# Turning the first mixer's sparse-attention queries and keys through VectorE and memory

## The chip, the cores and the metric

The kernel runs on one core of one Trainium2 chip. A core has five engines with queues of their own: TensorE (PE, matrix products into PSUM; PEld is its weight load), VectorE (DVE), ScalarE (ACT), GpSimd (POOL) and SyncE (SP, which issues transfers). The metric is the device time of one launch in microseconds, as a median of runs: 1248.22 us before, from runs of 1247.68, 1248.22 and 1251.99 us.

## The reference

A decoder trunk of two layers over 256 tokens of width 1024, in float32. Each layer is

```
x <- x + 1/2 * SwiGLU(RMSNorm(x))
h  = RMSNorm(x);  z = h @ W_in
  A: stick-breaking attention (8 heads)
  B: multi-head latent attention, MLA (8 heads of 64 + 32)
  C: native sparse attention, NSA (8 query heads of 64, 2 key groups)
y  = sum_i sigmoid(gate_i(h)) * (branch_i @ P_i)
x <- x + y @ W_out
x <- x + 1/2 * SwiGLU(RMSNorm(x))
```

Branch C is what the change touches. Its queries (512 columns of z), its selected keys (128) and its window keys (128) are each divided by their root mean square per head of 64, multiplied by a gain and rotated by position. Three attentions then use the queries: over 15 compressed keys, over the selected blocks and over a window. At 256 tokens all four blocks of 64 are selected and the window of 512 reaches over everything, so the last two are causal attentions with different keys.

## The kernel before

The 256 tokens lie as two row blocks of 128 (`NT = 2`, t = 0 and 1). Every matrix product in full precision is made of three products of a high and a low half (`mm3`, L588 to L590): ScalarE copies a value to a rounded type (the high half), VectorE subtracts (the low half). Weights go the same way (L1042, L1044). They arrive as slabs of 128 x 1024 through SP.

A layer is `ffn`, `mixer`, `ffn`. In the mixer the order of the work on TensorE, VectorE and ScalarE is written out by a planner (`Planner.run`): some twenty Python generators ask for an engine, with a cost, a latency, the events they depend on and the buffers they need, and the planner always emits the request that can start first, shifted by a fixed number per generator (`HOLDS`). The engines then run their lists in order. A request with the engine "-" costs nothing and takes only buffers or events. The costs are estimates in the code; transfers are estimated by a constant that is added to an event's time. POOL's transfers stand in POOL's list in the order in which they are emitted, and POOL also computes the powers for the root mean squares (L595).

The queries and keys of branch C lie in `nx[t]`, 128 tokens x 768 (eight query heads, then two selected and two window keys of 64). `nsa_prep` normalises and rotates them there (L1760 to L1780). For the attention products they must lie with the head's 64 numbers on the partitions and the tokens along the row. `nsa_T` does this for each row block: ScalarE writes a copy `kd` in which every key stands twice (L1888), so that a pair of query heads, which sits on partitions 0 to 63 and 64 to 127, finds its key on both halves; TensorE transposes the four query pairs (L1893) and the four doubled keys (L1902) against an identity into PSUM; ScalarE and VectorE split the results into `nq` and `nk` (L1068, L1070 in `t_split`). It waits for `ev_mqk`, the last MLA transposes, because `nq` and `nk` are taken from the ring of six big tiles (tag `hy`) that also holds MLA's `mq` and `mk`. The readers are `cmp_scores` (the product of `nq` with the compressed keys, L588 to L590 acc<-nq) and `nsa_scores` (L2036).

MLA already has another way of turning: `turn` (L1245) lets VectorE transpose a row block in place in squares of 32 x 32 and POOL write it to memory in four transfers (L1247), and `turned` (L1255) reads it back into a half tile `st` with the wanted rows on the partitions. The list `by_dve` says where: in the first mixer for `mk`, in the second for `mq` and `mk`. Half tiles come from a ring of seven (`TH_BUFS`, planner's `s_th`), which also holds gates, outputs and the copies `kd`.

Of the kernel before, what the change touches and what calls it, by code (L numbers as in the profile page):

```python
# [10 lines left out]
F = mybir.dt.float32  # L11
# [6 lines left out]
S = 256  # L18
# [3 lines left out]
NT = 2  # L22
# [203 lines left out]
def event():  # L226
    return Tok(None)
# [80 lines left out]
def use_v(n, *deps, slots=()):  # L308

    return "V", 0.065 + 0.00106 * n, 0.15 + 0.00106 * n, deps, slots  # L310
# [7 lines left out]
def use_a(n, *deps, slots=()):  # L318

    return "A", 0.085 + 0.00085 * n, 0.19 + 0.00085 * n, deps, slots  # L320
# [13 lines left out]
def use_t(count, *deps, slots=()):  # L334

    o = 0.2 + count * 0.109
    return "P", o, o + 0.2, deps, slots


def use_g(us, *deps, slots=()):  # L340

    return "G", us, us, deps, slots
# [29 lines left out]
def decoder_trunk(ctx, tc, xt_in, wts, lcon, cst, out, depth=DEPTH):  # L372
# [8 lines left out]
    dp = ctx.enter_context(tc.tile_pool(name="dp", bufs=1, space=bass.MemoryType.DRAM))  # L381
# [6 lines left out]
    def tp_tile():  # L388
        return pb.tile([128, 512], F, tag="ps", name="tp")
# [4 lines left out]
    def big_tile(name, dt=F, shape=(128, D)):  # L394
        return hp.tile(list(shape), dt, tag="hy", name=name, bufs=6)
# [196 lines left out]
    def rstd(ss, inv, w=1, p=128):  # L592
        r = sm.tile([128, 16], F, tag="rs", name="rs")
        nc.vector.tensor_scalar(ss[:p, :w], ss[:p, :w], inv, EPS, op0=OP.mult, op1=OP.add)
        nc.gpsimd.tensor_tensor(r[:p, :w], ss[:p, :w], mh[:p, :w], op=OP.pow)  # L595
        return r
# [351 lines left out]
    def mixer(l):  # L948
# [14 lines left out]
        def half_tile(name):  # L963
            return mp.tile([128, 512], F, tag="th", name=name, bufs=TH_BUFS)

        def tmp(n=768):
            return mp.tile([128, 768], F, tag="tmp", name="tmp", bufs=1)[:, :n]
# [9 lines left out]
        def bc(a, H):  # L977
            return a[:, None, :].to_broadcast([a.shape[0], H, a.shape[-1]])
# [17 lines left out]
        s_wf, s_wr, s_qk, s_th, s_tmp, s_of = Slots(4), Slots(WR_BUFS), Slots(4), Slots(TH_BUFS), Slots(1), Slots(1)  # L996

        def events(*n):
            return [events(*n[1:]) for _ in range(n[0])] if n else event()
# [65 lines left out]
        def t_split(hi, lo, src, n, k):  # L1065

            k = yield use_a(n, k)
            nc.scalar.activation(hi, src, AF.Copy)  # L1068
            k = yield use_v(n, k)
            nc.vector.tensor_sub(lo, src, hi)  # L1070
            return k
# [170 lines left out]
        def turn(x, t, dst, n, k):  # L1242

            k = yield "V", 0.065 + 0.00116 * n, 0.15 + 0.00116 * n, (k,), ()
            nc.vector.transpose(x[:, 0:n], x[:, 0:n])  # L1245
            for i in range(4):
                nc.gpsimd.dma_start(dst[:, :, t * 128 + 32 * i:t * 128 + 32 * (i + 1)],  # L1247
                                    x[32 * i:32 * (i + 1), 0:n].rearrange("b (m a) -> b m a", a=32))
            return Tok(k.t + 6.0)

        def turned(dst, parts):

            st = half_tile("st")
            for r, m, step, c in parts:
                nc.gpsimd.dma_start(st[32 * r:32 * (r + 1), c * S:(c + 2) * S].rearrange("b (j n) -> b j n", j=2),  # L1255
                                    dst[:, m:m + step + 1:step, :])
            return st
# [125 lines left out]
        side = {"_uq": side_uq, "_ukv": side_ukv, "w1_slab": lambda: compress()}  # L1383

        nx = [mp.tile([128, 768], F, name=f"nx{t}") for t in range(NT)]
        zc = []
        ev_nx, ev_zc, ev_v0 = events(NT, 2), events(NT), events(NT)

        def ev_nq(t, acc, k):
            k = yield use_a(512, k)  # L1390
# [364 lines left out]
        def nsa_prep():  # L1755
            for t in range(NT):
                x = nx[t].rearrange("p (h d) -> p h d", h=12)
                k = yield use_a(768, *ev_nx[t], slots=(s_tmp,))
                sq = tmp()
                nc.scalar.activation(sq, nx[t], AF.Square)  # L1760
                k = yield use_v(768, k)
                ss = sm.tile([128, 16], F, tag="ss", name="ss")
                nc.vector.tensor_reduce(ss[:, 0:12], sq.rearrange("p (h d) -> p h d", h=12), axis=AX.X, op=OP.add)
                k = yield "V", 0.07, 0.15, (k,), ()
                r = rstd(ss, 1.0 / 64, w=12)
                k = yield use_g(2.5, k)
                k = yield use_v(768, k)
                nc.vector.tensor_tensor(x, x, r[:, 0:12, None].to_broadcast([128, 12, 64]), op=OP.mult)
                b = tmp().rearrange("p (h d) -> p h d", h=12)
                for nm, hs_ in (("nq", slice(0, 8)), ("nk", slice(8, 12))):  # L1770
                    n = 64 * (hs_.stop - hs_.start)
                    xh, bh, H = x[:, hs_], b[:, hs_], hs_.stop - hs_.start
                    c, s_ = tab[nm][0][:, t, :], tab[nm][1][:, t, :]
                    for o, i in ((0, 32), (32, 0)):
                        k1 = yield use_v(n // 2, k)
                        nc.vector.tensor_tensor(bh[:, :, o:o + 32], xh[:, :, i:i + 32], bc(s_[:, o:o + 32], H), op=OP.mult)
                    k1 = yield use_v(n, k1)
                    nc.vector.tensor_tensor(xh, xh, bc(c, H), op=OP.mult)
                    k = yield use_v(n, k1)
                    nc.vector.tensor_tensor(xh, xh, bh, op=OP.add)  # L1780
                s_tmp.put(k)
                ev_prep[t].set(k)

        def gates():
# [95 lines left out]
        nq = tuple(big_tile("nq", R, (128, 4, S)) for _ in range(2))  # L1880
        nk = tuple(big_tile("nk", R, (128, 2, 2, NT, 128)) for _ in range(2))
        ev_nT = events(NT)

        def nsa_T():
            for t in range(NT):
                k = yield use_a(512, ev_prep[t], slots=(s_th,))
                kd = half_tile("kd").rearrange("p (a r d) -> p a r d", a=4, r=2)
                nc.scalar.activation(kd, nx[t][:, 512:768].rearrange("p (a d) -> p a d", a=4)[:, :, None, :]  # L1888
                                     .to_broadcast([128, 4, 2, 64]), AF.Copy)
                kt = yield use_t(4, ev_prep[t], *((*ev_mq, *ev_mk) if all(by_dve) else (ev_mqk,)), slots=(s_tp,))  # L1890
                tp = tp_tile()
                for p in range(4):
                    nc.tensor.transpose(tp[:, p * 128:(p + 1) * 128], nx[t][:, p * 128:(p + 1) * 128], ident)  # L1893
                ts = slice(t * 128, (t + 1) * 128)
                kt = yield from t_split(nq[0][:, :, ts], nq[1][:, :, ts], tp.rearrange("p (a b) -> p a b", a=4), 512, kt)
                s_tp.put(kt)
                k = yield use_t(4, k, slots=(s_tp,))
                tp = tp_tile()
                for g in range(2):
                    for sw in range(2):  # L1900
                        i = 2 * g + sw
                        nc.tensor.transpose(tp[:, i * 128:(i + 1) * 128],  # L1902
                                            kd[:, 2 * sw + g].rearrange("p a d -> p (a d)"), ident)
                s_th.put(k)
                k = yield from t_split(nk[0][:, :, :, t, :], nk[1][:, :, :, t, :],
                                       tp.rearrange("p (g s k) -> p g s k", g=2, s=2), 512, k)
                s_tp.put(k)
                ev_nT[t].set(k)

        def flat(pair):  # L1910
            return tuple(q.rearrange("p g r n -> p (g r n)") for q in pair)
# [230 lines left out]
        for th, hold in zip((scales(), tables(), sb_T(), sb_scores(), sb_pv(), cmp_in(), nsa_prep(), gates(), mla_T(),  # L2142
                             mla_scores(), mla_P(), mla_pv(), nsa_T(), k_chain(), v_chain(), cmp_scores(), nsa_scores(),
                             nsa_P(), nsa_pv(), bulk()), HOLDS):
            spawn(th, hold)
# [18 lines left out]
    for l in range(depth):  # L2164
        ffn(l, 0)
        mixer(l)
        ffn(l, 2)
# [35 lines left out]
```

## Time and profile before

| | |
|---|---|
| median of three runs | 1248.22 us |
| the profiled execution | 1249.25 us |
| its span | 1247.4 us |
| TensorE busy | 1239.0 us |
| VectorE busy | 943.6 us |
| ScalarE busy | 789.0 us |
| POOL busy | 155.5 us |
| granted TensorE clock | 1.00 |

The span is the part of the execution that the profiler's rows cover. A row of the kind "line, engine, operation, out<-in, x count" gives the least, median and greatest duration in ns. In the waits the engine and line that stood still come first, then the one that released it, then the sum in us, the number of times and the longest. The first mixer lies at about 190 to 445 us of the span, the second at about 810 to 1064 us.

### The profile page before, as it was taken

The page shows a single profiled execution, that of the slowest core. Times are in us where ns is not written, and L with a number is a line of the kernel's source. Part 1 is how long each engine was busy: PE and PEld are TensorE (multiplying, and loading weights), DVE is VectorE, ACT ScalarE, POOL GpSimd, SP SyncE. Part 2 cuts the span into 40 slices and gives each one's busy share as a digit, 9 for nine tenths or more (in the row PEclk, how much of TensorE's full clock was granted, in tenths as well). Part 3 has the DMA queues.
Part 4 walks back from the last instruction along what each step waited for, and adds up shares of the span by engine and source line. Part 5 has one row for each costly group of instructions (what it writes and reads, how often), then busy time and mean ns, then how long its engine had stood idle before and what let it go on. Part 6 is the DMA issues. An engine that isn't in the chain of part 4 may idle for free.

```text
span 1247.4 us, 26169 instructions
## 1 busy us (share of the span) xinstructions
PE 1239.0 (99%) x9314; PEld 1158.8 (93%) x9314; DVE 943.6 (76%) x1961; ACT 789.0 (63%) x1633; POOL 155.5 (12%) x250
## 2 busy tenths in 40 slices
PE   9999999999999999999999999999999999999998
PEld 8999999888878899999999999998888889999987
DVE  7876668988898777766677776689968987776644
ACT  6665557787887566655465565577757775565542
POOL 0021201231000001211001121013330000023000
PEclk9999999999999999999999999999999999999999
DMA  8899985667645568999758999666896556677753
GB/s 273 288 328 327 334 270 184 196 209 245 207 126 182 158 218 260 319 322 339 233 196 272 330 328 324 213 211 191 280 323 236 159 157 185 189 211 244 220 169 119
DMA packets 157218, 298.59 MB, mean 239 GB/s; under 512 B 21472, under 2 KB 24416, under 8 KB 157088
## 3 DMA queue, kind: packets, MB, share of 16 engines
q1 hardware_dynamic: 143872, 258.64, 64.8%
q0 software_dynamic: 13216, 38.29, 8.4%
q8 instruction: 73, 1.20, 0.4%
q14 instruction: 57, 0.47, 0.1%
HBM read 258.32 MB, written 38.01 MB: 238 GB/s over the span
## 4 chain that ended last, share of the span: by engine, by line
PE 94%; ACT 2%; DVE 2%; DMA 1%; issue 1%; SPq 0%; DVEq 0%; ACTq 0%
PE acc L779 13%; PE acc L778 13%; PE acc L780 12%; PE acc L588 9%; PE acc L590 9%; PE acc L589 9%; PE acc L669 6%; PE acc L670 6%; PE acc L668 6%; PE acc L1204 1%; PE acc L1206 1%; PE acc L1205 1%; DMA raw<-in_wts 1%; PE att L2036 1%; ACT wf L1632 1%; PE tp L2047 1%
## 5 line engine op out<-in xcount | busy, mean ns | idle before, releaser
L536 DVE TENSOR_TENSOR vlo<-raw,vhi 128x512 fp32r<-128x512 f32 x452 | 292.6, 686 | 82.6 <-ACT vhi L535 80.4
L778 PE MATMUL acc<-hThi,vhi 128*128 128x256 f32 x1280 | 353.4, 276 | 0.0
L780 PE MATMUL acc<-hThi,vlo 128*128 128x256 f32 x1280 | 353.4, 276 | 0.0
L779 PE MATMUL acc<-hTlo,vhi 128*128 128x256 f32 x1280 | 353.4, 276 | 0.0
L535 ACT ACTIVATE vhi<-raw 128x512 fp32r<-128x512 f32 x452 | 263.5, 622 | 134.9 <-DMA raw<-in_wts 36.0
L778 PEld LDWEIGHTS acc<-hThi,vhi 128*128 128x128 f32 x1280 | 240.3, 188 | 0.0
L780 PEld LDWEIGHTS acc<-hThi,vlo 128*128 128x128 f32 x1280 | 240.2, 188 | 0.0
L779 PEld LDWEIGHTS acc<-hTlo,vhi 128*128 128x128 f32 x1280 | 240.2, 188 | 0.0
L1044 DVE TENSOR_TENSOR wlo<-raw,whi 128x512 fp32r<-128x512 f32 x216 | 141.1, 680 | 30.4 <-ACT whi L1042 28.7
L1042 ACT ACTIVATE whi<-raw 128x512 fp32r<-128x512 f32 x216 | 124.8, 616 | 47.6 <-PE acc L590 17.2
L670 PE MATMUL acc<-gh,vlo 128*128 128x256 f32 x528 | 145.7, 276 | 0.0
L668 PE MATMUL acc<-gh,vhi 128*128 128x256 f32 x528 | 145.7, 276 | 0.0
L669 PE MATMUL acc<-gl,vhi 128*128 128x256 f32 x528 | 145.7, 276 | 0.0
L588 PE MATMUL acc<-whi,hThi 128*128 128x512 f32 (+2 forms) x352 | 138.1, 392 | 0.0
L590 PE MATMUL acc<-whi,hTlo 128*128 128x512 f32 (+2 forms) x352 | 133.6, 380 | 0.2 <-DVE hTlo L610 0.2
L589 PE MATMUL acc<-wlo,hThi 128*128 128x512 f32 (+2 forms) x352 | 133.3, 379 | 0.0
L554 ACT ACTIVATE ehi<-eraw 128x512 fp32r<-128x512 f32 x60 | 37.9, 632 | 107.3 <-DMA eraw<-in_wts 105.1
L536 DVE TENSOR_TENSOR wlo<-raw,whi 128x512 fp32r<-128x512 f32 (+2 forms) x109 | 70.0, 678 | 45.7 <-ACT whi L535 45.5
L555 DVE TENSOR_TENSOR elo<-eraw,ehi 128x512 fp32r<-128x512 f32 x60 | 41.4, 690 | 81.0 <-ACT ehi L554 80.8
L535 ACT ACTIVATE whi<-raw 128x512 fp32r<-128x512 f32 (+2 forms) x109 | 63.1, 617 | 57.9 <-PE acc L590 26.4
L668 PEld LDWEIGHTS acc<-gh,vhi 128*128 128x128 f32 x528 | 99.1, 188 | 0.0
L669 PEld LDWEIGHTS acc<-gl,vhi 128*128 128x128 f32 x528 | 99.1, 188 | 0.0
(348 smaller groups left out, 2560.1 us busy)
## 6 DMA issues: line engine op xcount, KB each, us to landing
raw<-in_wts SPq DMA_DIRECT2D x764, 256.0 KB, 3.6
eraw<-in_wts SPq DMA_DIRECT2D x60, 256.0 KB, 5.5
early<-ehi POOLq DMA_DIRECT2D x60, 256.0 KB, 4.2
early<-elo POOLq DMA_DIRECT2D x60, 256.0 KB, 4.8
whi<-early SPq DMA_DIRECT2D x60, 256.0 KB, 4.4
wlo<-early SPq DMA_DIRECT2D x60, 256.0 KB, 4.6
st<-md POOLq DMA_DIRECT2D x36, 64.0 KB, 5.1
xd<-x SPq DMA_DIRECT2D x4, 512.0 KB, 2.6
```

The costliest lines, as they stand in the source:

```text
L535: nc.scalar.activation(hi[:, q], raw[:, o:o + g], AF.Copy)
L536: last_lo[0] = nc.vector.tensor_tensor(lo[:, q], raw[:, o:o + g], hi[:, q], op=OP.subtract).ins
L588: nc.tensor.matmul(o, a[0], b[0], start=start, stop=False, **kw)
L589: nc.tensor.matmul(o, a[0], b[1], start=False, stop=False, **kw)
L590: nc.tensor.matmul(o, a[1], b[0], start=False, stop=stop, **kw)
L668: nc.tensor.matmul(o, sl[0][:, w], h, start=k == 0 and c == 0, stop=False)
L669: nc.tensor.matmul(o, sl[0][:, w], l_, start=False, stop=False)
L670: nc.tensor.matmul(o, sl[1][:, w], h, start=False, stop=k == kts - 1 and c == 1)
L778: nc.tensor.matmul(o, sl[0][:, w], h, start=k == 0 and c == 0, stop=False)
L779: nc.tensor.matmul(o, sl[0][:, w], l_, start=False, stop=False)
L780: nc.tensor.matmul(o, sl[1][:, w], h, start=False, stop=k == KT - 1 and c == 1)
L1044: nc.vector.tensor_tensor(hl[1][:, c:c + m], raw[:, :m], hl[0][:, c:c + m], op=OP.subtract)
```

## The change

In the first mixer (`l == 0`) a tensor `nd` in memory is added, 32 x 24 x 256. When a row block of `nx` is prepared, VectorE transposes it in place in squares of 32 and POOL writes it to `nd` (`turn`, 768 columns, four transfers of 96 KB each). The loop of `nsa_T` with `kd` and the transposes on TensorE runs no more there. In its place `n_back` makes four loads one behind another, two for the queries and two for the keys: a half tile is filled by four transfers of 32 partitions (64 KB each, `turned`), and `t_split` writes `nq` or `nk` from it. The doubling of the keys is done by reading the same rows of `nd` twice (`r % 2`). Each load waits for the writes of both row blocks, and the wait for `ev_mqk` is gone. All four loads together set the event `ev_nT` for both row blocks. The second mixer is as before.

```
+        nd = dp.tile([32, 24, S], F, tag="nd", name="nd") if l == 0 else None
...
+                if nd is not None:
+                    k = yield from turn(nx[t], t, nd, 768, k)
+                    ev_nd[t].set(k)
...
+        def n_back(what):
+            for i in range(2):
+                k = yield "-", 0.0, 0.0, tuple(ev_nd), (s_th,)
+                if what is nq:
+                    st = turned(nd, [(r, 8 * i + r, 4, 0) for r in range(4)])
+                    src, dst = st.rearrange("p (a n) -> p a n", a=2), [q[:, 2 * i:2 * i + 2] for q in nq]
+                else:
+                    st = turned(nd, [(r, 16 + 4 * i + r % 2, 2, 0) for r in range(4)])
+                    src = st.rearrange("p (g t k) -> p g t k", g=2, t=NT)
+                    dst = [q[:, :, i] for q in nk]
+                k = yield from t_split(dst[0], dst[1], src, 512, Tok(k.t + 5.0))
+                s_th.put(k)
+                ev_back[what is nq][i].set(k)
...
         def nsa_T():
-            for t in range(NT):
+            for t in range(NT if nd is None else 0):
...
+            if nd is not None:
+                yield from n_back(nq)
+                yield from n_back(nk)
+                for ev in ev_nT:
+                    ev.set(Tok(max(e.t for x in ev_back for e in x)))
```

More of the change, by code (lines that the diff above doesn't have):

```diff
@@ L1385, in mixer @@
         nx = [mp.tile([128, 768], F, name=f"nx{t}") for t in range(NT)]
+        nd = dp.tile([32, 24, S], F, tag="nd", name="nd") if l == 0 else None
         zc = []
-        ev_nx, ev_zc, ev_v0 = events(NT, 2), events(NT), events(NT)
+        ev_nx, ev_zc, ev_v0, ev_nd = events(NT, 2), events(NT), events(NT), events(NT)
         def ev_nq(t, acc, k):
@@ L1882, in mixer @@
         ev_nT = events(NT)
+        def n_back(what):
[11 more added lines that the diff above has]
+                ev_back[what is nq][i].set(k)
+        ev_back = events(2, 2)
         def nsa_T():
-            for t in range(NT):
+            for t in range(NT if nd is None else 0):
                 k = yield use_a(512, ev_prep[t], slots=(s_th,))
```

## The prediction

> **What bounds the kernel now.** I read first the page's busy times and the chain of waits, then the stretches of both mixers, then who TensorE waited for between 240 and 345 us, and last the rows of each tile that the edit touches.
>
> ```profile
> span 1247.4 us, 26169 instructions
> PE 1239.0 (99%) x9314; PEld 1158.8 (93%) x9314; DVE 943.6 (76%) x1961; ACT 789.0 (63%) x1633; POOL 155.5 (12%) x250
> ...
> PE 94%; ACT 2%; DVE 2%; DMA 1%; issue 1%; SPq 0%; DVEq 0%; ACTq 0%
> ```
>
> TensorE is busy for all but 8.4 of 1247.4 us and is 94% of the chain. A microsecond taken from TensorE's queue is therefore worth up to a microsecond; one taken from another engine is worth something only if TensorE waits for it. In the first mixer it hardly does (columns: stretch, its length, then busy us of PE, PEld, DVE, ACT, POOL, granted clock, DMA share, GB/s):
>
> ```profile
> 280.00:300.00 20.00, 20.00 (x125) 17.86 (x124) 18.54 (x44) 14.36 (x32) 6.62 (x10) 1.00 0.80 263
> 300.00:320.00 20.00, 20.00 (x144) 17.61 (x144) 15.83 (x49) 16.97 (x47) 0.00 (x0) 1.00 0.75 236
> 320.00:345.00 25.00, 24.42 (x173) 19.88 (x172) 22.77 (x61) 20.70 (x53) 0.94 (x1) 1.00 0.54 174
> ...
> sum 240.00, PE 239.26 PEld 205.61 DVE 205.89 ACT 181.20 POOL 27.32; mean PE 34.18 PEld 29.37 DVE 29.41 ACT 25.89 POOL 3.90
> ...
> PE tp L1945 <- DVE wf L1940: 0.3, 1, 0.3
> PE tp L1673 <- ACT wf L1664: 0.2, 1, 0.2
> ```
>
> From 200 to 440 us TensorE is idle for 0.74 us, and between 240 and 345 us it waits twice, 0.5 us in all, neither time for what the edit touches. So the edit cannot free more than the TensorE work that it takes out and those 0.74 us.
>
> **Taken from TensorE: 16 transposes.** They stand in four groups of four: nx at 324.37 and 327.57, kd at 325.76 and 336.94. The modelled duration of one (272 ns) overlaps its neighbours, so I take the time from a group's start to the next matmul's start.
>
> ```profile
> 324.14 0.40 PE L590 MATMUL acc<-whi,hTlo 128*128 128x512 f32 x1
> 324.37 0.60 PE L1893 MATMUL tp<-ident,nx 128*128 128x128 f32 x4
> 324.73 0.27 PE L588 MATMUL acc<-w,hvh 128*64 128x64 f32 x1
> ...
> 327.57 0.60 PE L1893 MATMUL tp<-ident,nx 128*128 128x128 f32 x4
> 327.93 0.48 PE L588 MATMUL acc<-whi,hThi 128*128 128x512 f32 x1
> 328.25 0.40 PE L589 MATMUL acc<-wlo,hThi 128*128 128x512 f32 x1
> 328.48 0.39 PE L590 MATMUL acc<-whi,hTlo 128*128 128x512 f32 x1
> ...
> 340.49 0.39 PE L588 MATMUL acc<-nq,zkh 128*128 128x256 f32 x1
> ```
>
> One group takes 0.36 us, and the matmul behind it 0.32 in place of the usual 0.23 (328.48 less 328.25), so 0.45 in all: 4 x 0.45 = 1.8. One of the four stands ahead of small matmuls, where less is lost, so I take **-1.7 us**.
>
> **ScalarE, VectorE and the two copies.** Removed are the two doubled copies kd; the four splits now read a loaded tile instead of a PSUM bank; added are two VectorE transposes of a row block, the same instruction that turns mk already.
>
> ```profile
> L1888 ACT ACTIVATE kd<-nx x4: 620/632/633, 281.5 to 918.8; 128x512 f32<-128x512 f32 x4
> L1068 ACT ACTIVATE nq<-tp x4: 577/597/599, 325.0 to 920.6; 128x512 fp32r<-128x512 f32 x4
> L1070 DVE TENSOR_TENSOR nq<-tp,nq x4: 674/687/693, 325.6 to 921.5; 128x512 fp32r<-128x512 f32 x4
> ...
> L1068 ACT ACTIVATE qk<-st x4: 614/618/625, 287.2 to 322.6; 96x512 fp32r<-96x512 f32 x4
> L1070 DVE TENSOR_TENSOR qk<-st,qk x4: 677/682/690, 290.2 to 324.2; 96x512 fp32r<-96x512 f32 x4
> ...
> L1245 DVE STREAM_TRANSPOSE mk<-mk x4: 970/972/980, 247.6 to 891.7; 128x768 f32<-128x768 f32 x4
> ```
>
> ScalarE: 2 x 0.632 less, 4 x (0.618 - 0.597) more, so -1.2 us. VectorE: 2 x 0.972 more and the splits equal, so +1.9 us. Both are costed at nothing on the path: TensorE's own queue covers them, and it does not wait there now. If that cover were gone, VectorE's 1.9 us would be the price; it is 93% busy from 280 to 300 us, where the first transpose falls, but only 79% in the next 20 us, so a delay of 1 us is made up there. The doubled copy of the first row block held one of the seven half tiles from 281.5 us until its transposes at 325.76; the new loads hold one at a time, so that ring gets no tighter.
>
> **POOL and the transfers.** Eight writes of 96 KB and sixteen reads of 64 KB are added, all issued by POOL. Their rows are those of mk's turn in this mixer:
>
> ```profile
> L1247 POOL DMA_DIRECT2D md<-mk x8: 694/735/789, 248.9 to 263.9; - x8
> md<-mk POOLq DMA_DIRECT2D x8, 96.0 KB, 2.6
> DMA to landing us min/median/max: 2.4/2.8/6.1
> ...
> L1255 POOL DMA_DIRECT2D st<-md x12: 533/533/605, 271.9 to 297.8; - x12
> DMA to landing us min/median/max: 2.1/4.1/5.1
> ...
> 296.67 1.65 POOL L1255 DMA_DIRECT2D st<-md  x3 [4.49 <-DVE y L1452]
> 326.53 0.94 POOL L595 TENSOR_TENSOR rs<-ss,mh 64x1 f32<-64x1 f32 x1 [28.21 <-DVE ss L594]
> 330.21 0.27 DVE L1928 TENSOR_SCALAR wf<-acc,rs 64x64 f32<-64x64 f32 x1
> ```
>
> (The first landing row is mk's in both mixers, 2.4 to 6.1; the second is st's in this one.) Issuing costs POOL 8 x 0.735 + 16 x 0.533 = 14.4 us, in a stretch where it now does nothing from 298 to 326 us. What queues behind a waiting read on POOL is the load for MLA's last head pair, now issued at 296.67 and first read 26 us later (the last st split, 322.6), and the power of the compressed keys at 326.53. Behind that power stands VectorE's L1928; its slack is 330.21 - 327.47 = 2.7 us, and four issues in front of the power are 2.1 us. Both are hidden, the second barely.
>
> [...]
>
> **The new wait.** The loads go one behind another: each takes a half tile, is read, split by ScalarE and VectorE, and only then comes the next.
>
> ```profile
> 299.72 0.42 DVE L1780 TENSOR_TENSOR nx<-nx,tmp 128x256 f32<-128x256 f32 x1
> ```
>
> The second row block is ready at 300.14. Then: transpose 0.97, issues 4 x 0.735 = 2.94, landing 2.6, so 306.65 us in memory. Each of the four trips: issues 4 x 0.533 = 2.13, landing 4.1, splits 0.62 + 0.68, so 7.53. Queries are there at 321.7 and keys at 306.65 + 4 x 7.53 = **336.8 us**. The first matmul that reads them stands at 340.49, and 3 of the 4 groups removed lie ahead of it plus the last at 336.94, so it moves to about 338.8. By medians the margin is 2 us. With the longest landings seen (6.1 once, 5.1 four times) the keys come at 336.8 + 3.5 + 4 x 1.0 = 344.3, and TensorE, which runs its list in order, would wait 5.5 us. With the shortest (2.1) they come at 328.6 and nothing waits.
>
> The smaller cost is ScalarE's. The planner puts each split 5.0 us behind its load (the constant in n_back), where issue and landing come to 2.13 + 4.1 = 6.2; ScalarE then stands still for about 1.2 us in front of each, 4.9 us in four, with softmax and weight splits queued behind it. It is idle 3.0 and 4.3 us in the two stretches from 300 to 345, so most of it fits. The second mixer shows what such waits can do, because there mq too goes through memory and its transposes are gone:
>
> ```profile
> ACT qk L1068 <- PE att L589: 5.6, 1, 5.6
> ...
> ACT qk L1068 <- DMA st<-md: 2.3, 1, 2.3
> ...
> 900.00:920.00 20.00, 18.18 (x118) 15.55 (x117) 15.76 (x42) 14.50 (x34) 8.72 (x13) 1.00 0.98 311
> ...
> L1126 PE MATMUL tp<-ident,wf x2: 272/272/272, 201.5 to 201.6; 128*128 128x128 f32 x2
> L670 PE MATMUL acc<-yT,wlo x64: 276/276/288, 422.3 to 444.7; 128*128 128x256 f32 x64
> ...
> L1126 PE MATMUL tp<-ident,wf x2: 272/272/273, 820.5 to 820.6; 128*128 128x128 f32 x2
> L670 PE MATMUL acc<-yT,wlo x64: 276/276/288, 1041.2 to 1063.7; 128*128 128x256 f32 x64
> ```
>
> ScalarE waits 7.9 us there around loaded tiles and TensorE is idle 1.82 us in that stretch, 0.23 of it. The two mixers take the same time from the row-scale transposes to the output projection: 422.3 - 201.5 = 220.8 and 1041.2 - 820.5 = 220.7 us, although the second has sixteen transposes less. There the saving was given back. For this edit 0.23 x 4.9 = **+1.1 us**; the bounds are 0 (early landings) and 5.5 (keys late at the first score matmul). I take 1.1, nearer to zero, because DMA is 54 to 75% busy here and was 98% there.
>
> [...]
>
> **Sum.** -1.7 + 1.1 = -0.6 us. The profiled execution took 1249.25 us (1.85 of it outside the span), 1.0 over the median of the three runs, 1248.22. So its own time becomes 1248.65, and the median about **1247.6**. The planner writes the order of this mixer out anew with the edit; neighbours will change places, which I price at nothing, since all but 0.74 us of TensorE's time there is work.
>
> **The rivals.**
>
> *Full gain, 0.22.* The loads land early or ScalarE's idle time swallows the waits: -1.7, and with the mixer's 0.74 us of idle gone too, -2.4, so 1246.5 to 1245.8. For it: no TensorE wait in this mixer is for a loaded tile today. Against it: the second mixer.
>
> *Keys late, 0.20.* The first score matmul waits for the keys, whose four trips are serial. A wait begins when the chain is 2.0 us longer than by medians, and the kernel gets slower once it is 3.7 us longer (2.0 of margin and the 1.7 saved). With every read at 5.1 and a write landing of 4.4, between the median and the longest, it is 5.8 us longer and the result is +2.1, so 1250.3; with the longest write too it is +3.8, so 1252.0. ScalarE's waits are not added, since they only use up part of the same wait. For it: medians already leave little. Against it: DMA is only 54% busy from 320 to 345 us.
>
> *A buffer not free, 0.06.* Queries and keys lie in the ring of six big tiles, in places that mq and mk leave; the old code waited for MLA's last transposes, the new code does not.
>
> ```profile
> 316.76 0.60 PE L1712 MATMUL tp<-ident,mq 128*96 128x128 f32 x4
> ```
>
> The first query split could come at 306.65 + 6.2 = 312.9. If its tile is one of mq's, ScalarE stands until 317.1, 4.2 us, and with all of it passed on the result is -1.7 + 1.1 + 4.2 = +3.6, so 1251.8. Against it: mk's places are free by 270 us and serve the queries, and by the sum the keys' first split is due at 327.
>
> *The forecast, 0.52:* a change of -1.5 to +0.5 us, 1246.7 to 1248.7.
>
> **How the numbers follow.** What a measurement of this kernel can tell from no change is about 0.5%, 6.2 us; no case reaches -6.2, as 2.4 is all that can be gained, and +6.2 needs two of the bad cases together. That gives faster 0.02, slower 0.05, same 0.93. The range runs from the full gain to the late keys, 1245.8 to 1252.0; the shown runs spread over 4.3 us, so I reach 1 us lower, and 0.5 higher: 1244.8 to 1252.5.
>
> **What would show it.** L1893 and L1902 with 8 instances each in place of 16, kd with 2; L1245 with two rows of nx near 282 and 301 us; the sixteen reads between 306 and 335 us with issues near 0.53 us; ScalarE waiting for st about 1 us four times; the first acc<-nq matmul near 339 us, with no TensorE wait in front of it. The step fails if that matmul waits for nk, if the issues lengthen, or if TensorE's idle time between 200 and 440 us grows by over 1.7 us.

## The result and the profile after

The changed kernel takes 1258.38 us, a median of six runs from 1256.76 to 1261.20 us; the kernel before took 1248.56 us, a median of six from 1247.68 to 1251.99 us. The ratio is 1.0082, with a 95% interval of 1.0071 to 1.0093: slower by about 10 us, where 0.6 us less had been forecast. The time lies above the range, too. The profiled execution of the changed kernel has a span of 1256.5 us.

The page's busy times and its chain of waits, changed kernel (engine, busy time, share, instructions):

```profile
span 1256.5 us, 26189 instructions
PE 1240.9 (99%) x9298; PEld 1160.2 (92%) x9298; DVE 946.2 (75%) x1962; ACT 789.0 (63%) x1632; POOL 170.1 (14%) x274
PE 93%; ACT 3%; DMA 2%; DVE 1%; issue 0%; SPq 0%; POOL 0%; ACTq 0%
```

The sixteen transposes are gone (9314 to 9298 matmuls), POOL has its 24 transfers more, and ScalarE and VectorE are about as busy as before. TensorE is busy 1.9 us longer although it has less to do, and the span is 9.1 us longer.

The rows of the two matmul groups that stand at both ends of the mixer, and the stretches of the mixer (stretch, length, busy us of PE, PEld, DVE, ACT, POOL, granted clock, DMA share, GB/s), changed kernel:

```profile
L1126 PE MATMUL tp<-ident,wf x2: 272/272/273, 201.5 to 201.6; 128*128 128x128 f32 x2
L670 PE MATMUL acc<-yT,wlo x64: 276/276/282, 432.5 to 455.0; 128*128 128x256 f32 x64
...
300.00:320.00 20.00, 19.19 (x139) 16.66 (x138) 12.42 (x32) 13.77 (x36) 9.29 (x17) 1.00 0.83 241
320.00:345.00 25.00, 18.13 (x106) 14.57 (x106) 18.86 (x57) 16.47 (x46) 4.53 (x8) 0.80 0.56 171
...
sum 250.00, PE 240.57 PEld 205.27 DVE 207.23 ACT 179.97 POOL 41.36; mean PE 48.11 PEld 41.05 DVE 41.45 ACT 35.99 POOL 8.27
```

The sum of the same five stretches from 200 to 450 us, kernel before:

```profile
sum 250.00, PE 249.26 PEld 215.61 DVE 214.92 ACT 189.82 POOL 27.32; mean PE 49.85 PEld 43.12 DVE 42.98 ACT 37.96 POOL 5.46
```

The first mixer, from the row-scale transposes to the last product of the output projection, took 444.7 - 201.5 = 243.2 us and now takes 455.0 - 201.5 = 253.5 us. That is 10.3 us more, where the whole span grew by 9.1 us: the loss lies in this mixer. TensorE's idle time from 200 to 450 us went from 0.74 to 9.43 us, so 8.7 of the 10.3 us are idle time, most of it between 320 and 345 us. What TensorE waited for there, and what ScalarE waited for from 300 to 345 us (engine, line, releaser: us in all, times, longest), changed kernel:

```profile
PE tp L1674 <- DVE wf L1663: 4.4, 1, 4.4
PE tp L1674 <- ACT wf L1665: 2.4, 1, 2.4
PE acc L589 <- DMA wlo<-early: 0.8, 1, 0.8
...
ACT nq L1068 <- DMA st<-nd: 7.9, 2, 4.8
ACT nk L1068 <- DMA st<-nd: 0.8, 1, 0.8
```

None of TensorE's waits names a query, a key or the tensor `nd`. It waits for `wf` of L1663 and L1665, which are the softmax probabilities of another branch, MLA, scaled by VectorE or ScalarE before TensorE transposes them (L1674); the 0.8 us is for a load of weights. How a late load gets there is seen in the order of time, changed kernel, rows of the timelines of POOL, ScalarE, VectorE and TensorE (start, duration, engine, instruction, and in brackets the idle time ahead of it and what ended it):

```profile
302.05 0.95 DVE L1245 STREAM_TRANSPOSE nx<-nx 128x768 f32<-128x768 f32 x1
304.67 2.87 POOL L1247 DMA_DIRECT2D nd<-nx  x4 [11.97 <-DVE small L1793]
310.36 2.15 POOL L1255 DMA_DIRECT2D st<-nd  x4 [2.83 <-ACT wf L1665]
...
313.28 0.69 ACT L1439 ACTIVATE th<-acc,rn 128x512 f32<-128x512 f32 x1
318.74 0.63 ACT L1068 ACTIVATE nq<-st 128x512 fp32r<-128x512 f32 x1 [4.78 <-DMA st<-nd]
324.17 0.63 ACT L1068 ACTIVATE nq<-st 128x512 fp32r<-128x512 f32 x1 [3.13 <-DMA st<-nd]
...
319.40 0.69 DVE L1070 TENSOR_TENSOR nq<-st,nq 128x512 fp32r<-128x512 f32 x1 [5.45 <-ACT nq L1068]
325.51 0.28 DVE L1858 TENSOR_TENSOR wf<-acc,wf 30x128 f32<-30x128 f32 x1 [2.56 <-ACT wf L1856]
327.64 0.29 DVE L1663 TENSOR_SCALAR wf<-wf,su 128x128 f32<-128x128 f32 x1
...
328.08 0.45 PE L1674 MATMUL tp<-ident,wf 128*128 128x128 f32 x1 [4.45 <-DVE wf L1663]
330.95 0.69 PE L1674 MATMUL tp<-ident,wf 128*128 128x128 f32 x2 [2.42 <-ACT wf L1665]
```

ScalarE comes to the first query split in its list at 313.97 us (313.28 + 0.69) and the load lands at about 318.7, so everything behind the split stands for 4.78 us. VectorE, whose low half of the same split comes next in its own list, stands for 5.45. ScalarE stands a second time, for 3.13 us, until 324.17; behind that split is L1856, for which VectorE waits 2.56 us, and behind VectorE's L1858 comes L1663, for which TensorE waits 4.45 us. TensorE had lived on work handed to it earlier until about 323.6.

The later reads did not leave POOL at once, either. POOL's waits for landings from 300 to 345 us, and three pieces of the chain that ended last (start, duration, what), changed kernel:

```profile
POOL st L1255 <- DMA st<-nd: 4.1, 4, 1.5
...
311.45 6.80 DMA st<-nd
...
318.53 5.54 DMA st<-nd
...
324.35 5.41 DMA st<-nd
```

POOL stood four times, 4.1 us in all, until an earlier read had landed. Counted in its list, the read issued at 318.53 us is the eighth transfer after that of 311.45, and the one of 324.35 the eighth after that of 318.53; each was issued 0.3 us after the earlier one had landed. Two of these waits (1.53 and 1.33 us) lie between the four reads of the second query load, which went out from 314.07 to 318.53 us. Together they are 2.9 us, nearly as long as ScalarE's second wait of 3.13. That the one makes most of the other is argued from the trace; no run took POOL's standing away by itself, and run 7 below has 1.8 us of it without a loss.

The second part of the loss is the clock. Stretches of 5 us of the changed kernel, columns as above:

```profile
325.00:330.00 5.00, 0.45 (x1) 0.18 (x1) 4.41 (x14) 4.22 (x16) 0.00 (x0) 0.61 0.69 220
330.00:335.00 5.00, 4.05 (x11) 2.86 (x12) 3.41 (x8) 3.08 (x8) 0.00 (x0) 0.50 0.33 107
335.00:340.00 5.00, 5.00 (x35) 4.49 (x34) 4.07 (x15) 2.37 (x8) 0.88 (x1) 0.86 0.18 57
```

After the long waits the granted clock is 0.61, 0.50 and 0.86. By (1 - clock) x busy time that costs 0.2 + 2.0 + 0.7 = 2.9 us, as an estimate. With 8.7 us of idle time and 1.7 us of transposes saved this makes 8.7 + 2.9 - 1.7 = 9.9 us, where 10.3 were measured.

### The profile page after: what moved, and what is told of

The parts are those of the page before. It is cut to its first block, busy times and chain, and to the rows that moved or that the text cites. A ratio compares the mean times of both kernels' runs of the same rounds, so it can differ in the third digit from the quotient of the medians.

```text
span 1256.5 us, 26189 instructions
## 1 busy us (share of the span) xinstructions
PE 1240.9 (99%) x9298; PEld 1160.2 (92%) x9298; DVE 946.2 (75%) x1962; ACT 789.0 (63%) x1632; POOL 170.1 (14%) x274
## 2 busy tenths in 40 slices
DMA packets 158115, 300.44 MB, mean 239 GB/s; under 512 B 21856, under 2 KB 24800, under 8 KB 157984
## 4 chain that ended last, share of the span: by engine, by line
PE 93%; ACT 3%; DMA 2%; DVE 1%; issue 0%; SPq 0%; POOL 0%; ACTq 0%
PE acc L779 12%; PE acc L780 12%; PE acc L778 12%; PE acc L588 9%; PE acc L590 9%; PE acc L589 9%; PE acc L669 6%; PE acc L670 6%; PE acc L668 6%; DMA st<-nd 1%; PE acc L1204 1%; PE acc L1205 1%; PE acc L1206 1%; ACT wf L1665 1%; ACT wf L1633 1%; PE tp L2072 1%
## 5 line engine op out<-in xcount | busy, mean ns | idle before, releaser
L670 PEld LDWEIGHTS acc<-gh,vlo 128*128 128x128 f32 x528 | 99.1, 188 | 0.0
```

What stands on the lines that cost most here:

```text
L670: nc.tensor.matmul(o, sl[1][:, w], h, start=False, stop=k == kts - 1 and c == 1)
```

## The experiments

Two theories went in. **Theory 1:** ScalarE's waits in front of late loads are the whole loss; TensorE gets them almost one to one, and what makes them is that the planner counts 5.0 us from a load's first issue to its split. **Theory 2:** it is the extra transfers themselves (their traffic, POOL's issuing, the new order that the planner writes), and the waits only show it. Theory 1 says that the same transfers with later splits run as before; theory 2 says that they stay slow. All ratios are against the kernel before, run on the same chip beside them; waits are ScalarE's on loads of `nd` from 300 to 345 us and idle time is TensorE's from 200 to 450 us, both from the profiled execution. In runs 8 and 11 the waits include 0.8 and 0.7 us in front of a split that reads a load of `nd`, which the profile puts down to another transfer (weights, `md`):

| run | what | us | ratio, 95% interval | waits | idle |
|---|---|---|---|---|---|
| - | before | 1248.56 | - | 0 | 0.74 |
| - | after | 1258.38 | 1.0082, 1.0071 to 1.0093 | 8.7 | 9.43 |
| 1 | splits 7.0 us behind the load | 1252.70 | 1.0036, 1.0023 to 1.0049 | 6.6 | 6.11 |
| 2 | 9.0 us behind it | 1255.71 | 1.0052, 1.0037 to 1.0068 | 4.6 | 6.61 |
| 3 | reads issued by SP | 1255.80 | 1.0055, 1.0040 to 1.0070 | 6.1 | 7.65 |
| 4 | before, without the 16 transposes | 1247.23 | 0.9983, 0.9971 to 0.9994 | 0 | 1.48 |
| 5 | before, with the transfers | 1258.46 | 1.0083, 1.0068 to 1.0098 | 9.3 | 9.00 |
| 6 | as 5, each load read | 1265.73 | 1.0139, 1.0124 to 1.0154 | 9.7 | 12.55 |
| 7 | loads by row block, 9.0 us | 1248.89 | 0.9998, 0.9988 to 1.0007 | 0.4 | 1.34 |
| 8 | reads issued by SP, 8.0 us | 1253.21 | 1.0047, 1.0031 to 1.0064 | 5.4 | 5.44 |
| 9 | all four loads at once, 9.0 us | 1259.68 | 1.0095, 1.0077 to 1.0114 | 4.9 | 9.54 |
| 10 | as 7, 7.0 us | 1254.32 | 1.0050, 1.0038 to 1.0062 | 8.2 | 6.11 |
| 11 | as 7, 12.0 us | 1246.81 | 0.9990, 0.9982 to 0.9999 | 0.7 | 2.33 |

**1 and 2. The splits later in the list.** One constant of the changed kernel:

```
-                k = yield from t_split(dst[0], dst[1], src, 512, Tok(k.t + 5.0))
+                k = yield from t_split(dst[0], dst[1], src, 512, Tok(k.t + 7.0))   # run 2: 9.0
```

> The changed kernel with one constant altered: the planner counts 7.0 us instead of 5.0 from taking the half tile to the split that reads it. Theory 1 (ScalarE runs its list in order and stands in front of a split whose load has not landed; everything behind it comes late to TensorE): ScalarE's waits for st<-nd, 8.7 us in the changed kernel (4.8 + 3.1 + 0.8), fall by about 2 for the first and more for the later ones, to about 4; TensorE's idle time between 200 and 440 us, 9.4 us in the changed kernel, falls to about 4; time about 1253. Theory 2 (the transfers themselves, or the new order of work around them, cost the time): nothing moves, 1257 to 1259.

> The changed kernel with 9.0 us instead of 5.0 counted for each load. Theory 1: ScalarE's waits for st<-nd under 2 us, TensorE idle in the first mixer under 2 us, time 1247 to 1250. Against that, the four loads still come one behind another, and each is 4 us longer in the plan, so the keys may come after 340 us and the first score matmul may then wait: up to 1253. Theory 2: 1256 or more.

ScalarE's waits, run 1:

```profile
ACT nq L1068 <- DMA st<-nd: 4.6, 2, 2.3
ACT nk L1068 <- DMA st<-nd: 2.0, 2, 1.3
```

and TensorE's, run 2:

```profile
PE tp L1674 <- DVE su L2034: 3.2, 1, 3.2
PE att L589 <- DVE qk L1070: 1.6, 1, 1.6
PE att L588 <- ACT qk L1068: 1.0, 1, 1.0
```

With 7.0 us over half of the loss is gone (1.0082 to 1.0036), so the constant is a cause; the waits fell less than theory 1 had said, to 6.6 us and not to about 4. With 9.0 us the waits for `nd` shrink further, but the time does not: TensorE now also waits for `qk`, MLA's last pair, whose load stands behind the reads of `nd` on POOL. TensorE's longest wait there, 3.2 us, ends at 357 us behind L2034 in the softmax over the compressed keys and was not followed. The constant by itself does not bring the time of before back, so theory 1 in its plain form does not hold.

**3. Another queue for the reads.** 

```
-        def turned(dst, parts):
+        def turned(dst, parts, q=nc.gpsimd):
...
-                nc.gpsimd.dma_start(st[32 * r:32 * (r + 1), ...
+                q.dma_start(st[32 * r:32 * (r + 1), ...        # nc.sync for nd
```

> The changed kernel, but the sixteen reads of nd are issued by SP instead of POOL. Theory 1, with the lateness coming from POOL's issue and landing (2.1 + 6.8 us for the first load): landings as the weights' on SP, about 3.5 us, ScalarE's wait for the first load falls from 4.8 to about 2 us, time 1250 to 1254; but on SP the reads wait for the writes' landing with weight loads queued behind them, which could cost as much. Theory 2 (the transfers' load on memory and the order of work): 1256 or more.

The sixteen reads among the transfers from 200 to 345 us (count, size of one, median us from issue to landing), changed kernel first, then run 3:

```profile
st<-nd POOLq DMA_DIRECT2D x16, 64.0 KB, 5.5
```

```profile
st<-nd SPq DMA_DIRECT2D x16, 64.0 KB, 3.6
```

SP's reads land 1.9 us earlier by the median, and the first query split (at 315.37 us) no longer waits, where 2 us of waiting had been expected to stay. But SP issued six loads of weights before the reads of the second query load, which went out only from 316.67 us, and the second split stands 4.0 us for them. A third of the loss goes. The queue is a part of the lateness, not all of it.

**4. The saving by itself.** The kernel before, without the sixteen transposes of the first mixer: the splits read `nx` and `kd` where they lie, and the planner's costs stay.

```
-                tp = tp_tile()
-                for p in range(4):
+                tp = nx[t][:, 0:512] if l == 0 else tp_tile()
+                for p in range(4 if l else 0):
```

> The kernel before with the 16 transposes of the first mixer left out; queries and keys are split straight from nx and kd, so they are not turned. It prices the saving alone, with nothing put in its place. If the saving is what the trace's gaps give: 1.7 us less, about 1246.8. If TensorE would only wait elsewhere: no change, 1248.5.

0.9983 is 2.1 us less, with an interval of 0.7 to 3.6 us. The 1.7 us that the prediction put on the transposes fits in it.

**5 and 6. The transfers by themselves.** The kernel before with all 24 transfers added, of `nx` as it lies (no VectorE transpose), into half tiles that nobody reads; each is given back 6.3 us after it was taken. In run 6 ScalarE copies each loaded tile and VectorE adds it to itself, with nothing made of the result.

```
+        def loads():
+            for i in range(4 if nd is not None else 0):
+                k = yield "-", 0.0, 0.0, tuple(ev_nd), (s_th,)
...                                                      # turned(nd, ...)
+                k = yield "-", 0.0, 0.0, (Tok(k.t + 6.3),), ()
+                s_th.put(k)
```

> The kernel before, transposes and doubled copies kept, plus the eight writes of nx (not turned, so VectorE has nothing more to do) and the sixteen reads into half tiles, which no instruction reads. It prices the transfers and POOL's part alone. Theory 1 (the price is ScalarE standing in line in front of a load): no ScalarE wait for st<-nd exists, so 1248.5, at most 1 more from half tiles that are held. Theory 2 (the transfers press on memory and on POOL): 1254 or more.

> As e5, and each loaded tile is read: a ScalarE copy of 512 columns onto itself, put 5.0 us behind the load as the changed kernel does, and a VectorE sum behind it; nothing uses the result. Queries and keys still come from TensorE's transposes. Theory 1: ScalarE waits 8 to 9 us for st<-nd as in the changed kernel, TensorE idles 6 to 8 us more, time 1257 to 1260, although nothing was taken away. Theory 2: as e5.

ScalarE's waits on loads of `nd` in run 5, and what TensorE waited for:

```profile
ACT th L1440 <- DMA st<-nd: 5.5, 1, 5.5
ACT ou L1499 <- DMA st<-nd: 3.8, 1, 3.8
...
PE tp L1675 <- ACT wf L1666: 7.3, 1, 7.3
```

Run 5 is as slow as the changed kernel, and theory 1 had said that it would be as fast as before. But the rows show waits of the same kind: the half tile had been promised to the next writer (`th`, `ou`) before the load into it had landed, and ScalarE stood in front of that write. So run 5 does not separate the two theories; it shows that a load nobody reads can hold up an engine too, through the next owner of its buffer. Run 6 has the reader and the same late load. It takes 7 us more than run 5 (0.0056 x 1248.5), with waits only 0.4 us longer and 3.6 us more idle time; where the rest comes from was not followed.

ScalarE's waits, run 6:

```profile
ACT st L1925 <- DMA st<-nd: 9.7, 3, 6.2
```

**7, 10 and 11. The same transfers, cut by row block.** In place of two loads for all tokens of two query pairs and two for half of the keys, each load takes one row block: four query pairs or the four doubled keys of 128 tokens. It needs the writes of that block alone, so the first block's loads start while the second is still being prepared. The blocks ask separately, the keys' splits wait for `ev_mqk` as in the kernel before, and the time counted from load to split is 9.0, 7.0 or 12.0 us. Sizes, count and issuing engine of the transfers are those of the change.

```
+        def n_back(t):
+            w = slice(t * 128, (t + 1) * 128)
+            k = yield "-", 0.0, 0.0, (ev_nd[t],), (s_th,)
+            st = half_tile("st")
+            for r in range(4):
+                nc.gpsimd.dma_start(st[32 * r:32 * (r + 1)].rearrange("b (j n) -> b j n", j=4), nd[:, r:r + 13:4, w])
...                                       # split at k.t + LAND; keys: nd[:, m:m + 7:2, w], m = 16 + r % 2
-                yield from n_back(nq)
-                yield from n_back(nk)
+                spawn(n_back(1), 0.05)
+                yield from n_back(0)
```

> The changed kernel with the loads cut by row block: each brings the four query pairs, or the four doubled keys, of one block of 128 tokens, so the first block does not wait for the second; the two blocks run side by side; 9.0 us are counted per load, and the keys' splits wait for MLA's last transposes as in the kernel before. Theory 1: no ScalarE wait for st<-nd above 1 us, TensorE idle in the first mixer about 1 us, time 1246.5 to 1248.5, the saving of 1.7 us kept in part. Theory 2, since all transfers remain: 1254 or more.

> As e7 (loads by row block), 7.0 us counted instead of 9.0. Theory 1: the second block's query split may stand 1 to 2 us in front of its load, TensorE idles about that much more: 1248.5 to 1251.

> As e7, 12.0 us counted. No ScalarE wait for st<-nd; the keys are split later but still ahead of the first score matmul. TensorE idle in the first mixer about 1 us, time 1246.5 to 1249; if the saving of 1.7 us is kept it is below the kernel before.

What the transfers amount to and the sum of the mixer's stretches, run 7:

```profile
DMA packets 158115, 300.44 MB, mean 241 GB/s; under 512 B 21856, under 2 KB 24800, under 8 KB 157984
...
sum 250.00, PE 248.66 PEld 215.68 DVE 217.61 ACT 189.51 POOL 42.84; mean PE 49.73 PEld 43.14 DVE 43.52 ACT 37.90 POOL 8.57
```

ScalarE's wait in run 10, from its timeline:

```profile
303.35 0.63 ACT L1069 ACTIVATE nq<-st 128x512 fp32r<-128x512 f32 x1 [8.18 <-DMA st<-nd]
```

The packets and bytes of run 7 are the changed kernel's own (158115 and 300.44 MB), and its transfers of `nd` do not land earlier (writes and reads together, least, median and longest: 3.7, 5.3 and 6.5 us; 3.0, 4.9 and 6.8 in the changed kernel). Yet it takes the time of before, with 0.4 us of waits. Theory 2 falls as far as traffic, POOL's issuing and VectorE's transposes go, for all of them are in run 7. Run 7 stands 1.9 us above run 4 (0.0015 x 1248.5), so what they cost there is about what the transposes had given. Run 10 differs from run 7 by one constant, 2.0 us, and costs 6.2 us (0.0050 x 1248.5): a single wait of 8.18 us stands at the first block's split, where 1 to 2 us had been expected at the second's, and TensorE's idle time is 4.8 us longer than in run 7. ScalarE came to that split at 295.17 us (303.35 - 8.18), 0.3 us after the first of its reads was issued (294.83); why 2.0 us less moved the split that far was not followed. Run 11 counts 12.0 us, has 0.7 us of such waits, and comes out at 0.9990, 1.2 us under the kernel before; the interval leaves between 0.1 and 2.2 us. It is the only version with the change's transfers whose interval lies below the time of before, by less than the 0.5% that the prediction calls a difference.

**8 and 9. Neither half alone.** Run 8 is run 3 with 8.0 us counted. Run 9 keeps the changed kernel's four loads, but asks for all at once and counts 9.0 us, with the splits behind `ev_mqk`:

```
+                land = Tok(k.t + 9.0)
+                yield "-", 0.0, 0.0, (land, ev_mqk), ()
+                k = yield from t_split(dst[0], dst[1], src, 512, land)
...
-                yield from n_back(nq)
-                yield from n_back(nk)
+                for w in (nq, nk):
+                    for i in range(2):
+                        spawn(n_back(w, i), 0.05)
```

> The changed kernel with the reads issued by SP (as e3, landing 3.6 us in place of 4.9) and 8.0 us counted per load. Theory 1: ScalarE's waits, 6.1 us in e3, fall under 2 us and TensorE idles 2 to 4 us in the first mixer: 1249 to 1252. What may stay is the plan that puts the keys late. Theory 2: as e3, 1256.

> The changed kernel's own loads (halves of the queries or keys, both row blocks in each), but all four asked for at once instead of one behind another, 9.0 us counted and the splits put behind MLA's last transposes as in the kernel before. It tells the cut by row block in e7 apart from the time that the plan allows. If the time allowed is what counts: ScalarE's waits for st<-nd under 2 us, 1248 to 1251. If the first block's early load is needed: the four loads land in one burst after 306 us, MLA's last load stands behind them on POOL, and TensorE idles 4 us or more: 1252 to 1256.

Run 8 waits 4.6 us in front of the second query split and 0.8 in front of a key split, where under 2 us in all had been expected. Run 9's waits, and one that TensorE had there:

```profile
ACT nk L1068 <- DMA st<-nd: 4.9, 2, 3.2
ACT qk L1068 <- DMA st<-md: 1.0, 1, 1.0
...
PE acc L588 <- ACT hvh L1068: 3.8, 1, 3.8
```

Run 9 has run 7's constant and run 7's wait for `ev_mqk`, and is 11.9 us slower than before (0.0095 x 1248.5), more than had been expected. Sixteen reads asked for in one heap behind the second block's writes land late, and MLA's last load is issued behind them at 322.8 us; a second wait of TensorE, 3.2 us at L1519, was not followed. So 9.0 us without the cut (runs 2, 9) and the cut with only 7.0 us (run 10) leave 61% of the loss or more; both together (runs 7, 11) take it away. The cut with the 5.0 us of the change was not run.

Over all runs the waits and the added idle time go together, though not exactly: 8.7 us of waits and 8.7 of idle time in the changed kernel, 6.6 and 5.4 in run 1, 6.1 and 6.9 in run 3, 5.4 and 4.7 in run 8, 9.3 and 8.3 in run 5, 8.2 and 5.4 in run 10. Runs 2, 6 and 9 have 1 to 4 us more idle time than waits; in runs 2 and 9 the late load of `qk` comes in, the rest was not followed. No run that had over 4 us of these waits lost less than 4.5 us (0.0036 x 1248.5, run 1).

## Why the prediction was wrong, point by point

**The sixteen transposes, -1.7: right.** Run 4 measured -2.1 (-0.7 to -3.6). Three of the four groups, not one, stand ahead of small matmuls (at 324.73, 326.11 and 337.29 us), but the four groups alone take 1.42 us, so the size holds.

**VectorE and the issues' length: right.** The transposes take 0.95 us. In the changed kernel the issues cost what the rows of MLA's turn had said:

```profile
L1247 POOL DMA_DIRECT2D nd<-nx x8: 709/730/769, 285.8 to 306.8; - x8
L1255 POOL DMA_DIRECT2D st<-nd x16: 533/533/557, 310.4 to 324.4; - x16
```

The longest issue here is 0.77 us, where it was 0.79 in the kernel before. That POOL would stand 4.1 us between its issues was not in the prediction. The power at L595, priced as barely hidden, made no wait on TensorE.

**Landing, 4.1 us, and "DMA is 54 to 75% busy here": wrong.** That share was the kernel's before; the added transfers raised it in just the stretch where they had to land, from 0.93 and 0.76 (315 to 320 and 320 to 325 us, kernel before) to 1.06 and 1.03. The two stretches of 5 us around the first query load, changed kernel:

```profile
315.00:320.00 5.00, 4.19 (x38) 3.63 (x37) 0.59 (x1) 1.26 (x3) 1.79 (x5) 1.00 1.06 275
320.00:325.00 5.00, 3.63 (x16) 2.64 (x15) 2.90 (x11) 1.84 (x4) 3.64 (x7) 1.00 1.03 309
```

The share is that of the core's DMA engines, as the profile counts it; the reads' median landing is 5.5 us and the longest 6.8. The writes were late besides: the second block was ready at 300.5 us, nearly as predicted, but its transpose stood behind other work in VectorE's list until 302.05, and POOL began to write 1.7 us after its end. The first read came at 310.36 us, not at 306.65.

**The serial chain, keys at 336.8: wrong, and with it the rival "keys late".** The first product that reads queries or keys, changed kernel:

```profile
L588 PE MATMUL acc<-nq,zkh x4: 276/278/283, 350.7 to 351.9; 128*128 128x256 f32 x4
...
329.87 0.63 ACT L1068 ACTIVATE nk<-st 128x512 fp32r<-128x512 f32 x1 [0.76 <-DMA st<-nd]
```

The sixteen reads were issued from 310.4 to 324.4 us; a load does not wait for the split of the one before (the second began at 314.07, the first split at 318.74), but reads did follow one another through POOL's waits for landings, shown above. The last key split was written at about 331.4 us (VectorE's half starts at 330.77 and takes 0.67), 5 us earlier than the chain had it; the first reader of the queries came at 350.7, of the keys (L2061) at 354.6. The prediction watched for lateness at the reader of the data, and the loss came through the list of the engine that splits it. "A buffer not free" did not happen either: the first query split stood at 318.74, after `mq`'s last transposes, and waited for its load alone.

**The failed step: "0.23 x 4.9 = +1.1 us".** Both factors were too small, and a third term was missing. ScalarE waited 8.7 us, not 4.9: not four times 1.2 us, but 4.78, 3.13 and 0.76, because the writes were late, the landings were longer, its list had got to the first split at 313.97, and POOL had stood between the reads of the second load. TensorE's idle time grew by as much, 8.7 us, not by 0.23 of it: 6.9 us are the two waits for `wf` traced above and 0.8 us the wait for weights, which is not ScalarE's doing; the rest, a wait of 1.0 us at L1674 for `wr` among it, was not followed. The same kind of wait cost 4.7 to 8.7 us in runs 1, 3, 5, 8, 10 and the change.

The factor 0.23 was a misreading of the kernel before. It divides TensorE's 1.82 us of idle time from 900 to 920 us by 7.9 us of ScalarE's waits from 860 to 960. Only 2.3 of these are a wait for a load in that stretch. The other 5.6 us end later, are put down to TensorE itself, and cost it nothing; kernel before:

```profile
929.04 0.63 ACT L1068 ACTIVATE qk<-st 96x512 fp32r<-96x512 f32 x1 [5.59 <-PE att L589]
...
920.00:940.00 20.00, 20.00 (x136) 17.49 (x135) 11.77 (x37) 12.33 (x33) 4.74 (x9) 1.00 0.97 323
```

Set against the 2.3 us alone, 1.82 is 0.8 of it (of TensorE's waits there, 1.0 us is for `qk` itself and 0.7 us for `wf`): the second mixer did not hide its late load either, and with 0.8 the step would have given 3.9 us in place of 1.1, still under half of what came.

The third term is the lower clock after the idle time, estimated at 2.9 us, which was priced nowhere. With the two sizes read from this trace the step is 8.7 + 2.9 in place of 1.1, and the sum -1.7 + 11.6 = +9.9 us.

**"TensorE's own queue covers them": wrong in the way that it was read.** An idle time of 0.74 us before the change says that the lists fitted each other; it does not say how far ahead of TensorE the other engines ran. Here the cover held from 313.97, when ScalarE stopped, to about 323.6, and was gone when ScalarE and VectorE had been stopped a second time.

**"The planner writes the order anew, which I price at nothing": partly wrong.** The order fixes where the split stands in the list, and run 10 against run 7 shows 6.5 us (by the ratios, 0.0052 x 1248.5) between two lists made from constants 2.0 us apart. The change's transfers in the lists of runs 7 and 11 cost no more than the 2 us that the transposes gave.

What stays open: how much of run 7's success is the earlier start of the first block and how much the separate asking, how much of ScalarE's second wait is POOL's standing, and whether a constant under 5.0 us would have been worse, which was not tried.

## What to carry to other kernels

In a list that an engine runs in order, a transfer's estimated landing time is a place in the list, and an estimate that is too early stops everything behind it (ScalarE for 4.78 and 3.13 us here): price the whole wait as passed on to the bound engine unless the trace shows a reserve that is longer (8.7 us of waits came with 8.7 us more idle time). A factor read from another stretch has to set waits and idle time of the same moments against each other. Take the landing time from a stretch as full as the changed one will be (4.1 us by the median before the change, 5.5 after it), count the lower clock after waits of several microseconds (0.50 here after idle times of 4.45 and 2.42 us), and start the load as early as its first piece of data allows. The next owner of a buffer waits for a late load too, even where nobody reads it (5.5 and 3.8 us in run 5).

## What was not expected of the hardware

The clock: after one idle stretch of 4.45 us and one of 2.42 with a single matmul between them, the granted clock was 0.50 and recovered to 0.86 in the stretch from 335 to 340 us and to 1.00 in the next. In the stretch of 0.50 a 128x512 matmul came 0.42 us after its neighbour, where 0.23 is usual (the prediction's rows); two neighbours of the changed kernel:

```profile
332.72 0.63 PE L588 MATMUL acc<-whi,hThi 128*128 128x512 f32 x1
333.14 0.63 PE L589 MATMUL acc<-wlo,hThi 128*128 128x512 f32 x1
```

That is 333.14 - 332.72 = 0.42 us. From what length of idle time on the clock is lower, no run here shows.

The same sixteen reads of 64 KB landed in 5.5 us by the median when POOL issued them and in 3.6 when SP did (run 3), the one edit between the two kernels; the reads went out at other moments, too, so a part of the 1.9 us may come from that.
